# Query and key operands of two attention heads made on 128 partitions and put together by transfers

## The chip, the cores and the metric

The kernel runs on one core of a Trainium2 chip. The metric is the device time of one execution in microseconds (us), as the median of several runs. Times inside an execution come from one profiled execution; its span is counted from the first to the last instruction. TensorE is called PE, VectorE DVE, ScalarE ACT, GpSimd POOL and SyncE SP.

## The reference

One layer of a decoder with two kinds of attention side by side, for a sequence of 512 rows of width 1024, in float32:

```
h   = RMSNorm_pre(x)
[q_a|k_a|v_a|q_b|k_b|v_b] = h @ W_in
y_a = sliding-window attention with sinks + ALiBi   (8 query heads, 2 key/value heads, window 128)
y_b = differential attention + ALiBi                (4 heads, two 64-wide q/k each, 128-wide v)
x   = x + RMSNorm_post(concat(y_a, y_b) @ W_out)
x   = x + RMSNorm_post(W_down(gelu(g) * v)),  [g|v] = causal_dwconv3(RMSNorm_pre(x) @ W_up)
```

Scores are `q . k / 8 - slope * distance`, masked, then a softmax. All heads are 64 wide for queries and keys, so one projection of 128 columns holds two query heads, or the two keys of a differential head, or the two key heads of the window attention.

## The kernel before, in words

**Precision.** Every float32 matrix product is made from halves: an operand is rounded to a high part (`hi`, type float32r) and what is left is kept as a low part (`lo`). A general product takes three matmuls (hi·hi, lo·hi, hi·lo). In `split` and its like ACT makes the high part with a copy and DVE the low part with a subtraction.

**Scores.** `scores` (L387 to 390) makes a product of 64 channels with two matmuls instead of three, since PE has 128 rows: the query operand `q` holds in its 64 upper partitions the high part and in the 64 lower ones the low part of one head; the key operands `kh` and `kl` hold the high part, or the low part, of one head twice, in both halves. For the second head of a projection the high part lies in the lower partitions.

**How the operands are made.** A projection ends in `evac` (L340 to 346): DVE multiplies the sums by the reciprocal norms (L343), into a tile `pr` of 128 partitions (two heads of 64) and 512 columns, and hands it to one of two makers, each called once per head:

- `q_stack` (L369 to 375): ACT writes the scaled high part of 64 partitions (L373); DVE writes the scaled low part into the other 64 partitions (L374).
- `k_dup` (L377 to 385): ACT writes the high part of 64 partitions (L381), DVE the low part (L382); two transfers from SBUF to SBUF, issued by POOL (L383, L384, 64x512, 128 KB each), put the copies in the other 64 partitions.

`queries_a` and `keys_a` make the operands of the window attention (four query projections and one of keys), `queries_b` and `keys_b` those of the four differential heads (one of each per head). All operands come from a ring of 30 tiles of 128x512 (`a2`), taken and given back in order.

**What sets the order.** The attention is a list of steps: `swa_a` to `swa_c` for eight pairs of block and key head, then `diff_a` to `diff_e` for 16 pairs of head and block. Between steps `fill` takes pieces of work off a queue: the projections (`queue_projection`, L358 to 360, 24 matmuls each), the values (`queue_values`, L322 to 324) and later the output projection, so that PE has something to do while DVE and ACT work on the softmax. The framework then sorts the instructions of each engine by its own estimates, so that the order on an engine is not that of the text, and a small edit can move instructions in places that it does not touch. Each engine runs its list in order; an instruction that waits holds up all behind it on that engine.

**Other lines that are spoken of.** L389 and L390 are the two matmuls of `scores`. DVE reads the scores in L539 (window) and L417 (differential), and scales them in L428 and L554. L444 and L568 are transposes of the probabilities on PE. L195, L199 to L210 and L220 make and spread a row's norm (the power L201 on POOL, L210 on DVE, L220 on PE). L476 on DVE ends a differential head and frees its PSUM bank. L119 and L898 (ACT) with L120 and L899 (DVE) split weights. `post_a` takes the mean square of the new rows (L642, L649 on ACT, L629 to L631 on POOL) and scales them (L648, L656 on DVE); `post_b` transposes them (L664). From about 220 us on the feed-forward part runs, which the change's functions do not touch.

Of the kernel before, what the change touches and what calls it, by code (L numbers as in the profile page):

```python
# [10 lines left out]
F32 = mybir.dt.float32  # L11
F32R = mybir.dt.float32r
AF = mybir.ActivationFunctionType
ALU = mybir.AluOpType
PSUM = bass.MemoryType.PSUM

P = 128
# [4 lines left out]
DH = 64  # L22
# [10 lines left out]
T2, T4, T8, F2 = 30, 5, 3, 9  # L33


PAD = 72

WARM = 8

# [19 lines left out]
def fl(t):  # L59
    return t.bitcast(F32)  # L60
# [16 lines left out]
def hymba_layer(ctx, tc, x, st, wv, wqk, w_out, w_up, w_down, conv, cols, lam_in, sinks, gpost, gffn, gfin, out):  # L77
    nc = tc.nc
    TT = nc.vector.tensor_tensor
    STT = nc.vector.scalar_tensor_tensor  # L80
    ACT = nc.scalar.activation

    def pool(name, bufs=1, side="left", **kw):
        return tc.tile_pool(name=name, bufs=bufs, side=side, **kw)

    const = ctx.enter_context(pool("const"))
# [13 lines left out]
    a2 = Arena(wk, T2, [P, S], F32R, "a2")  # L100
# [3 lines left out]
    t2 = a2.get  # L104
# [34 lines left out]

    const.tile([P, PAD], F32, name="pad")  # L140
    cols_sb = const.tile([P, 16], F32, name="cols_sb")
# [31 lines left out]
    q = [(wqk[i], {}) for i in range(10)]  # L173
# [2 lines left out]
    nv = 2 + 2 * V_AFTER  # L176
    jobs += v[0:3] + q[0:nv] + v[3:6] + q[nv:10] + o + [(w, dict(big=True)) for w, kw in o[4::-1]]
    W = Stream(jobs, 2)

    ones_r = const.tile([P, P], F32R, name="ones_r")  # L180
    nc.vector.tensor_copy(ones_r, ones)
# [54 lines left out]
    for k in range(NK):  # L236
# [4 lines left out]
        else:  # L241
            t = f2.get(), f2.get()
# [8 lines left out]
    for k, (xr, wr, held) in enumerate(sts):  # L251
        ACT(hTh[k], xr, AF.Copy, scale=g_in(k))
        STT(hTl[k], xr, g_in(k), fl(hTh[k]), ALU.mult, ALU.subtract)
        h, l = t2(), t2()
        ACT(h[:, 0:384], wr, AF.Copy)
        TT(l[:, 0:384], wr, fl(h[:, 0:384]), op=ALU.subtract)
        for j in range(3):
            c = slice(j * P, (j + 1) * P)
# [12 lines left out]
    nc.sync.dma_start(lam_sb, lam_in)  # L271
    W.prepare(2)
    for t in range(NT):
# [35 lines left out]
    def queue_values(batch):  # L309
        st = {}  # L310

        def job(t, part):
            if t == 0 and part == 0:
                st["w"] = [W.next() for _ in range(3)]
            if part == 0:
# [32 lines left out]
    def queue_projection(done):  # L348
        st = {}

        def job(u):
            if u == 0:
                st["w"], st["o"] = W.next(), banks.get()
            h, l = st["w"]
# [11 lines left out]

    halves = [(slice(0, DH), slice(DH, P)), (slice(DH, P), slice(0, DH))]

    def q_stack(pr, half, scale):  # L369

        q = t2()
        a, b = halves[half]
        ACT(q[a], pr[a], AF.Copy, scale=scale)  # L373
        STT(q[b], pr[a], scale, fl(q[a]), ALU.mult, ALU.subtract)  # L374
        return q

    def k_dup(pr, half):  # L377

        kh, kl = t2(), t2()
        a, b = halves[half]  # L380
        ACT(kh[a], pr[a], AF.Copy)  # L381
        TT(kl[a], pr[a], fl(kh[a]), op=ALU.subtract)  # L382
        nc.gpsimd.dma_start(kh[b], kh[a])  # L383
        nc.gpsimd.dma_start(kl[b], kl[a])  # L384
        return kh, kl

    def scores(o, q, kd, qs, ks):  # L387
        kh, kl = kd
# [8 lines left out]
    kdb, qsb, pts, soft, ys, zq = {}, {}, {}, {}, {}, {}  # L397
    blocks = [[0, 1, 2, 3]] * 3 + [[2, 3, 0, 1]]

    def keys_b(h, pr):  # L400
        kdb[h] = [k_dup(pr, 0), k_dup(pr, 1)]

    def queries_b(h, pr):
        c = 0.125 * 2.0 ** (5 + h)
        qsb[h] = [q_stack(pr, 0, c), q_stack(pr, 1, c)]

    def diff_a(h, i):
        w = (i + 1) * P
# [78 lines left out]
    def mix(ts_, c, first, last, t):  # L487
        if t == ts_[0]:
            wmix[ts_, c] = kept.pop(c) if c in kept else W.next()
            if ts_ == (2, 3) and c > 4:  # L490
# [180 lines left out]
    kda, qa = [], []  # L671

    def keys_a(pr):
        kda.extend([k_dup(pr, 0), k_dup(pr, 1)])

    def queries_a(c, pr):
        qa.extend([q_stack(pr, 0, 0.125 * 2.0 ** c), q_stack(pr, 1, 0.125 * 2.0 ** (c + 1))])

    def queue_head(h):
        queue_projection(partial(keys_b, h))  # L680
        queue_projection(partial(queries_b, h))
# [27 lines left out]
    nc.gpsimd.tensor_scalar(g_sub, cols_sb[:, 12:13], DIFF_V ** 0.5 * (1.0 - LAMBDA_INIT), 0.0, op0=ALU.mult, op1=ALU.add)  # L709

    evac(st_ps[0], keys_a)
    for c in range(2):
        evac(st_ps[1 + c], partial(queries_a, c))
    queue_values(0)
    for c in range(2, 4):
        queue_projection(partial(queries_a, c))
# [9 lines left out]
    for m in range(2):  # L726
        nc.vector.tensor_tensor_reduce(out=lprod[:, m], in0=lam_sb[:, 2 * m], in1=lam_sb[:, 2 * m + 1],
                                       scale=1.0, scalar=0.0, op0=ALU.mult, op1=ALU.add,
# [33 lines left out]
    for n in range(2, len(steps) + DEP):  # L762
        if n < len(steps):
            h, i = steps[n]
# [79 lines left out]
    def sum_copy(q, n):  # L844
        name, b = (("U", B11), ("W", B12), ("V", B22), ("Z", B21))[n]
        sums[name, q] = dram.tile([P, D], F32, tag=f"{name}{q}", name=f"{name}{q}")
        tc.keep_in_program_order(nc.sync.dma_start(sums[name, q], w_down[q, b]))

    def sum_add(q, n):
        name, b = (("U", B12), ("W", B22), ("V", "U"), ("Z", "V"))[n]  # L850
        src = w_down[q, b] if isinstance(b, int) else sums[b, q]
        tc.keep_in_program_order(nc.gpsimd.dma_start(sums[name, q], src, accum_op=ALU.add, max_dma_last_dim=8192))
# [9 lines left out]
    for t, i, j in ((t11, 0, 0), (t21, 1, 0), (t22, 1, 1), (t12, 0, 1)):  # L862
        h, l = h_of(i, j)
# [224 lines left out]
    def get2():  # L1088
        return [banks.get(), banks.get()]
# [4 lines left out]
    a = get2()  # L1094
# [3 lines left out]
    c = get2()  # L1098
# [3 lines left out]
    b = get2()  # L1102
# [109 lines left out]
```

## Time and profile before

| | |
|---|---|
| median of 3 runs | 725.46 us (725.34 to 725.89) |
| the profiled execution | 724.03 us; its span 722.3 us |
| PE busy | 701.9 us (97%) |
| DVE busy | 625.1 us (87%) |
| ACT busy | 446.3 us (62%) |
| POOL busy | 70.0 us (10%) |
| transfers of L383 and L384 | 20, of 128.0 KB, 2.7 us from issue to landing in the median |

A busy engine was in an instruction; time spent on a semaphore or in handing a transfer to its queue is not counted. PE's matmuls overlap, so that in a timeline the distance between starts tells what one costs, and its own duration is longer. An idle time with an arrow names what ended it.

### The profile page before, as it was taken

To read this page: it belongs to the slowest core of one execution; us is meant where nothing else is said; L and a number is where in the kernel's file an instruction comes from. 1 tells how busy PE (TensorE), PEld (TensorE's weight loads), DVE (VectorE), ACT (ScalarE), POOL (GpSimd) and SP (SyncE) were. 2 spreads that over 40 slices of the span, in tenths; PEclk is the share of its full clock that TensorE was granted. 3 is DMA by queue.
4 is the path that set the end of the run, shared out by engine and by line. 5 is a ranking of instruction groups with operands and counts; after the bars stand their busy time and mean duration, and the time that the engine had idled before them with its cause. 6 is when DMAs were issued, how large, how long until landed. Compare 5 with 4: busy or idle time off the path is not lost.

```text
span 722.3 us, 11314 instructions
## 1 busy us (share of the span) xinstructions
PE 701.9 (97%) x4164; PEld 619.7 (86%) x4164; DVE 625.1 (87%) x1050; ACT 446.3 (62%) x790; POOL 70.0 (10%) x126
## 2 busy tenths in 40 slices
PE   8999999899998999999999999999999899999995
PEld 7888888688788889899999999999998788888884
DVE  6599979999785799999999899899987999988983
ACT  6698867677564455665575556557565666656661
POOL 2100102010322200000000000000000000000301
PEclk9999999999999999999999999999999999999998
DMA  8622223245667866887677686777864656677631
GB/s 305 228 87 59 85 87 95 73 117 166 194 231 269 206 154 190 249 212 214 182 193 212 181 245 179 213 185 190 229 164 145 237 184 203 191 249 255 210 117 58
DMA packets 33351, 130.83 MB, mean 181 GB/s; under 512 B 4752, under 2 KB 5776, under 8 KB 30736
## 3 DMA queue, kind: packets, MB, share of 16 engines
q1 hardware_dynamic: 28240, 107.57, 44.8%
q0 software_dynamic: 4480, 20.45, 15.3%
q10 hardware_dynamic: 576, 2.10, 0.7%
q8 instruction: 32, 0.52, 0.3%
q14 instruction: 23, 0.19, 0.1%
HBM read 123.29 MB, written 37.75 MB: 223 GB/s over the span
## 4 chain that ended last, share of the span: by engine, by line
PE 63%; DVE 5%; issue 1%; ACT 0%; POOL 0%; POOLq 0%; ACTq 0%; DVEq 0%
PE bank L940 10%; PE bank L942 10%; PE bank L941 9%; PE bank L1056 7%; PE bank L1057 7%; PE bank L1055 7%; PE bank L695 4%; PE bank L696 4%; PE bank L697 4%; DVE ct L832 1%; DVE ct L833 1%; DVE act L864 1%; DVE wlo L120 0%; DVE wlo L899 0%; PE bank L664 0%
## 5 line engine op out<-in xcount | busy, mean ns | idle before, releaser
L119 ACT ACTIVATE whi<-wr 128x1024 fp32r<-128x1024 f32 (+1 forms) x81 | 85.4, 1056 | 66.8 <-PE bank L1056 47.3
L120 DVE TENSOR_TENSOR wlo<-wr,whi 128x1024 fp32r<-128x1024 f32 (+1 forms) x81 | 98.5, 1217 | 19.9 <-ACT whi L119 19.3
L1056 PE MATMUL bank<-whi,al 128*128 128x512 f32 x224 | 87.3, 390 | 1.5 <-DVE al L394 1.5
L1055 PE MATMUL bank<-whi,ah 128*128 128x512 f32 x224 | 87.0, 390 | 0.4 <-ACT ah L393 0.4
L1057 PE MATMUL bank<-wlo,ah 128*128 128x512 f32 x224 | 87.2, 389 | 0.0
L898 ACT ACTIVATE whi<-wr 128x1024 fp32r<-128x1024 f32 x60 | 63.1, 1056 | 34.8 <-PE bank L696 15.5
L899 DVE TENSOR_TENSOR wlo<-wr,whi 128x1024 fp32r<-128x1024 f32 x60 | 73.1, 1219 | 0.6 <-ACT whi L898 0.6
L940 PE MATMUL bank<-hTh,whi 128*128 128x256 f32 x252 | 72.6, 289 | 0.7 <-ACT ub L959 0.5
L941 PE MATMUL bank<-hTl,whi 128*128 128x256 f32 x252 | 71.0, 282 | 0.0
L942 PE MATMUL bank<-hTh,wlo 128*128 128x256 f32 x252 | 70.4, 283 | 0.0
L695 PE MATMUL bank<-hTh,whi 128*128 128x512 f32 (+1 forms) x160 | 60.8, 380 | 0.0
L696 PE MATMUL bank<-hTl,whi 128*128 128x512 f32 (+1 forms) x160 | 60.7, 380 | 0.0
L697 PE MATMUL bank<-hTh,wlo 128*128 128x512 f32 (+1 forms) x160 | 60.7, 379 | 0.0
L898 ACT ACTIVATE whi<-sm 128x1024 fp32r<-128x1024 f32 (+1 forms) x42 | 34.7, 840 | 39.7 <-PE bank L941 19.0
L940 PEld LDWEIGHTS bank<-hTh,whi 128*128 128x128 f32 x252 | 48.1, 191 | 4.2 <-ACT ub L959 3.5
L1056 PEld LDWEIGHTS bank<-whi,al 128*128 128x128 f32 x224 | 42.0, 188 | 10.7 <-DVE al L394 1.9
L1055 PEld LDWEIGHTS bank<-whi,ah 128*128 128x128 f32 x224 | 42.0, 188 | 9.8 <-ACT ah L393 0.8
L899 DVE TENSOR_TENSOR wlo<-sm,whi 128x512 fp32r<-128x512 f32 (+1 forms) x42 | 39.9, 955 | 11.5 <-ACT whi L898 11.3
L1057 PEld LDWEIGHTS bank<-wlo,ah 128*128 128x128 f32 x224 | 42.1, 188 | 8.5
L941 PEld LDWEIGHTS bank<-hTl,whi 128*128 128x128 f32 x252 | 48.2, 191 | 0.5
L942 PEld LDWEIGHTS bank<-hTh,wlo 128*128 128x128 f32 x252 | 47.8, 191 | 0.0
L697 PEld LDWEIGHTS bank<-hTh,wlo 128*128 128x128 f32 x160 | 30.1, 188 | 5.9 <-DVE wlo L899 0.2
(266 smaller groups left out, 2017.7 us busy)
## 6 DMA issues: line engine op xcount, KB each, us to landing
wr<-in_w_up SPq DMA_DIRECT2D x64, 512.0 KB, 3.9
wr<-in_w_down SPq DMA_DIRECT2D x24, 512.0 KB, 4.3
wr<-in_w_out SPq DMA_DIRECT2D x13, 512.0 KB, 3.8
wr<-in_wqk SPq DMA_DIRECT2D x10, 512.0 KB, 3.7
Z<-in_w_down SPq DMA_DIRECT2D x8, 512.0 KB, 5.1
U<-in_w_down SPq DMA_DIRECT2D x8, 512.0 KB, 5.3
W<-in_w_down SPq DMA_DIRECT2D x8, 512.0 KB, 6.5
V<-in_w_down SPq DMA_DIRECT2D x8, 512.0 KB, 4.8
```

Source lines behind the costliest of these rows:

```text
L120: TT(l, r, fl(h), op=ALU.subtract)
L695: nc.tensor.matmul(u[:, c0:c1], lhsT=h[:, c], rhs=hTh[k][:, c0:c1], start=(k == 0), stop=False)
L696: nc.tensor.matmul(u[:, c0:c1], lhsT=h[:, c], rhs=hTl[k][:, c0:c1], start=False, stop=False)
L697: nc.tensor.matmul(u[:, c0:c1], lhsT=l[:, c], rhs=hTh[k][:, c0:c1], start=False, stop=(k == NK - 1))
L898: ACT(h[:, 0:n], src, AF.Copy)
L899: TT(l[:, 0:n], src, fl(h[:, 0:n]), op=ALU.subtract)
L940: nc.tensor.matmul(o[:, 0:H], lhsT=wh[:, c], rhs=rh[:, k], start=first and k == 0, stop=False, skip_group_check=True)
L941: nc.tensor.matmul(o[:, 0:H], lhsT=wh[:, c], rhs=rl[:, k], start=False, stop=False, skip_group_check=True)
L942: nc.tensor.matmul(o[:, 0:H], lhsT=wl[:, c], rhs=rh[:, k], start=False, stop=k == 3, skip_group_check=True)
L1055: nc.tensor.matmul(o, lhsT=ah[:, j, rs], rhs=wh[:, cs], start=first and j == 0, stop=False, skip_group_check=True)
L1056: nc.tensor.matmul(o, lhsT=al[:, j, rs], rhs=wh[:, cs], start=False, stop=False, skip_group_check=True)
L1057: nc.tensor.matmul(o, lhsT=ah[:, j, rs], rhs=wl[:, cs], start=False, stop=last and j == 1, skip_group_check=True)
```

## The change

For two heads at once: ACT writes the high part of all 128 partitions, once into each of the two operand tiles. DVE makes the low part of all 128 partitions in one subtraction. What has to lie in the other half is moved by transfers of 64 partitions that POOL issues: for queries two transfers of low parts out of a tile that is then given back, for keys four (high and low part of both heads), with one more ACT copy of the low part for the second operand. The scale of the window attention's queries now differs between the halves of an instruction, so it comes from a small constant tile, `qscale`, which eight memsets on POOL fill. A padding tile is made smaller by as much.

```diff
-PAD = 72
+PAD = 64
...
+    qscale = const.tile([P, 4], F32, name="qscale")
+    for c in range(4):
+        for m in range(2):
+            nc.gpsimd.memset(qscale[m * DH:(m + 1) * DH, c:c + 1], 0.125 * 2.0 ** (c + m))
...
-    def q_stack(pr, half, scale):
-
-        q = t2()
-        a, b = halves[half]
-        ACT(q[a], pr[a], AF.Copy, scale=scale)
-        STT(q[b], pr[a], scale, fl(q[a]), ALU.mult, ALU.subtract)
+    def q_stack(pr, scale):
+
+        (a, b), q, l = halves[0], (t2(), t2()), t2()
+        for t in q:
+            ACT(t, pr, AF.Copy, scale=scale)
+        STT(l, pr, scale, fl(q[0]), ALU.mult, ALU.subtract)
+        nc.gpsimd.dma_start(q[0][b], l[a])
+        nc.gpsimd.dma_start(q[1][a], l[b])
+        a2.free(l)
         return q
 
-    def k_dup(pr, half):
-
-        kh, kl = t2(), t2()
-        a, b = halves[half]
-        ACT(kh[a], pr[a], AF.Copy)
-        TT(kl[a], pr[a], fl(kh[a]), op=ALU.subtract)
-        nc.gpsimd.dma_start(kh[b], kh[a])
-        nc.gpsimd.dma_start(kl[b], kl[a])
-        return kh, kl
+    def k_dup(pr):
+
+        (a, b), kh, kl = halves[0], (t2(), t2()), (t2(), t2())
+        for t in kh:
+            ACT(t, pr, AF.Copy)
+        TT(kl[0], pr, fl(kh[0]), op=ALU.subtract)
+        ACT(kl[1], fl(kl[0]), AF.Copy)
+        for t in kh, kl:
+            nc.gpsimd.dma_start(t[0][b], t[0][a])
+            nc.gpsimd.dma_start(t[1][a], t[1][b])
+        return list(zip(kh, kl))
...
     def keys_b(h, pr):
-        kdb[h] = [k_dup(pr, 0), k_dup(pr, 1)]
+        kdb[h] = k_dup(pr)
...
-        qsb[h] = [q_stack(pr, 0, c), q_stack(pr, 1, c)]
+        qsb[h] = q_stack(pr, c)
...
-        kda.extend([k_dup(pr, 0), k_dup(pr, 1)])
+        kda.extend(k_dup(pr))
 
     def queries_a(c, pr):
-        qa.extend([q_stack(pr, 0, 0.125 * 2.0 ** c), q_stack(pr, 1, 0.125 * 2.0 ** (c + 1))])
+        qa.extend(q_stack(pr, qscale[:, c:c + 1]))
```

The lines behind the change have other numbers: in the listings L322 to L324 become L328 to L330, L358 to L360 become L364 to L366, L389 and L390 become L400 and L401, L444 becomes L455, and L649, L653 and L898 become L660, L664 and L909.

**First listing: PE at the start of the attention.** The matmuls with `hTh` and `hTl` make values; those of tiles `a2...` are the first scores: `a226_118` is the first key's high part, `a20_92` the first query operand. Before:

```order
L322 MATMUL bank2_86<-whi_401,hTh_177 128x320
L389 MATMUL bank5_89<-a226_118,a20_92 128x256
L389 MATMUL bank4_88<-a226_118,a20_92 128x256
L323 MATMUL bank2_86<-whi_401,hTl_178 128x320
L324 MATMUL bank2_86<-wlo_402,hTh_177 128x320
L322 MATMUL bank2_86<-whi_401,hTh_177 128x320
L323 MATMUL bank2_86<-whi_401,hTl_178 128x320
L324 MATMUL bank2_86<-wlo_402,hTh_177 128x320
L389 MATMUL bank6_90<-a226_118,a22_94 128x256
```
With the change:

```order
L328 MATMUL bank2_86<-whi_412,hTh_186 128x320
L329 MATMUL bank2_86<-whi_412,hTl_187 128x320
L330 MATMUL bank2_86<-wlo_413,hTh_186 128x320
L400 MATMUL bank5_89<-a226_118,a20_92 128x256
L400 MATMUL bank4_88<-a226_118,a20_92 128x256
L328 MATMUL bank7_91<-whi_318,hTh_186 128x320
L329 MATMUL bank7_91<-whi_318,hTl_187 128x320
L330 MATMUL bank7_91<-wlo_319,hTh_186 128x320
L401 MATMUL bank5_89<-a228_120,a20_92 128x256
```
The five matmuls on `bank2_86` that stood behind the first two scores stand ahead of them now. Behind these two come matmuls for other values, on `bank7_91`, and then the product with the key's low part (`a228_120`); the scores of the third query operand (`a22_94`) are later.

**Second listing: PE in differential head 2.** The matmuls with `hTh` and `whi` are those of the next projection; into `bank1_85` the first of them can only start when L476 has given that bank back. Before:

```order
L444 MATMUL bank3_87<-ident_149,a42_124 128x128 x4
L389 MATMUL bank2_86<-a226_118,a22_94 128x256
L390 MATMUL bank2_86<-a227_119,a22_94 128x256
L389 MATMUL bank4_88<-a226_118,a22_94 128x256
L390 MATMUL bank4_88<-a227_119,a22_94 128x256
L389 MATMUL bank5_89<-a24_96,a23_95 128x256
L390 MATMUL bank5_89<-a25_97,a23_95 128x256
L389 MATMUL bank6_90<-a24_96,a23_95 128x256
L390 MATMUL bank6_90<-a25_97,a23_95 128x256
L358 MATMUL bank1_85<-hTh_177,whi_1390 128x512
L359 MATMUL bank1_85<-hTl_178,whi_1390 128x512
```
With the change:

```order
L455 MATMUL bank3_87<-ident_149,a42_124 128x128 x4
L364 MATMUL bank1_85<-hTh_186,whi_1405 128x512
L365 MATMUL bank1_85<-hTl_187,whi_1405 128x512
L366 MATMUL bank1_85<-hTh_186,wlo_1406 128x512
L364 MATMUL bank1_85<-hTh_186,whi_1405 128x512
L400 MATMUL bank2_86<-a22_94,a28_100 128x256
L401 MATMUL bank2_86<-a27_99,a28_100 128x256
L400 MATMUL bank4_88<-a22_94,a28_100 128x256
L401 MATMUL bank4_88<-a27_99,a28_100 128x256
L365 MATMUL bank1_85<-hTl_187,whi_1405 128x512
L366 MATMUL bank1_85<-hTh_186,wlo_1406 128x512
```
Four of the projection's matmuls, which stood behind the first scores, stand ahead of them now, and two more between the first and the second query operand's.

**Third listing: ACT behind the attention.** L649 (L660) takes the squares of the new rows for `post_a`; L898 (L909) is a weight's split. Before:

```order
L898 ACTIVATE whi<-wr 128x1024
L649 ACTIVATE f_131,r_2151<-a_123 128x512
L649 ACTIVATE f_129,r_2151<-a_123 128x512
L653 DMA x_2156<-a_123 128x1024
L642 ACTIVATE f_128,r<-bank_85 128x512
```
With the change:

```order
L660 ACTIVATE f_131,r_2168<-a_123 128x512
L909 ACTIVATE whi<-wr 128x1024
L660 ACTIVATE f_129,r_2168<-a_123 128x512
L664 DMA x_2173<-a_123 128x1024
L653 ACTIVATE f_128,r<-bank_85 128x512
```
One of the two squares has moved ahead of the weight's split.

## Rows read from the trace of the kernel before

**Rows 1.** Busy time and share of each engine, from the page

```profile
PE 701.9 (97%) x4164; PEld 619.7 (86%) x4164; DVE 625.1 (87%) x1050; ACT 446.3 (62%) x790; POOL 70.0 (10%) x126
```

**Rows 2.** Stretch, its length, busy PE, PEld, DVE, ACT, POOL, clock, DMA share, GB/s

```profile
40.00:165.00 125.00, 122.00 (x658) 103.14 (x657) 114.77 (x307) 96.05 (x236) 13.10 (x28) 1.00 0.32 89
40.00:60.00 20.00, 20.00 (x115) 17.34 (x114) 19.27 (x56) 19.55 (x51) 0.00 (x0) 1.00 0.33 100
125.00:145.00 20.00, 18.09 (x91) 14.27 (x90) 18.86 (x49) 13.33 (x32) 3.08 (x7) 1.00 0.30 80
```

**Rows 3.** Groups by line and form: busy us, mean ns; idle before, releaser

```profile
L373 ACT ACTIVATE a<-f 64x512 fp32r<-64x512 f32 x16 | 10.0, 627 | 0.6 <-DVE f L343 0.4
L374 DVE SCALAR_TENSOR_TENSOR a<-f,a 64x512 fp32r<-64x512 f32 x16 | 11.0, 686 | 0.5
L394 DVE TENSOR_TENSOR al<-act,ah 128x512 fp32r<-128x512 f32 x48 | 32.8, 684 | 0.0
L252 ACT ACTIVATE hTh<-a,cols_sb 128x512 fp32r<-128x512 f32 x5 | 3.6, 723 | 4.2 <-DMA a<-in_st 4.2
L384 POOL DMA_DIRECT2D a<-a x10 | 5.1, 516 | 1.3 <-DVE a L382 0.6 <-issue 0.4 <-DVE a L554 0.2
```

**Rows 4.** Line L383, whole span: its transfers' time from issue to landing

```profile
DMA to landing us min/median/max: 2.2/2.7/4.0
```

**Rows 5.** Line L383, 71 to 76 us: the same

```profile
DMA to landing us min/median/max: 3.6/3.8/4.0
```

**Rows 6.** Timelines, 30 to 37 us: start, us, engine, line [idle before <-releaser]

```profile
31.93 1.39 DVE L382 TENSOR_TENSOR a<-f,a 64x512 fp32r<-64x512 f32 x2
31.79 1.32 POOL L383 DMA_DIRECT2D a<-a  x2 [6.78 <-ACT a L381]
34.37 0.48 PE L389 MATMUL bank<-a,a 128*128 128x256 f32 x2
36.90 0.38 PE L389 MATMUL bank<-a,a 128*128 128x256 f32 x1 [0.24 <-DVE m L539]
```

**Rows 7.** Timelines of DVE and PE, 57 to 59 us

```profile
57.27 0.69 DVE L374 SCALAR_TENSOR_TENSOR a<-f,a 64x512 fp32r<-64x512 f32 x1
58.19 0.28 PE L389 MATMUL bank<-a,a 128*128 128x256 f32 x1
```

**Rows 8.** Timelines of DVE and PE, 115 to 122 us

```profile
115.86 1.40 DVE L374 SCALAR_TENSOR_TENSOR a<-f,a 64x512 fp32r<-64x512 f32 x2
117.23 0.28 PE L389 MATMUL bank<-a,a 128*128 128x256 f32 x1
121.21 0.50 PE L220 MATMUL bank<-a,ones_r 128*128 128x512 f32 x1 [0.47 <-DVE a L210]
```

**Rows 9.** Timelines of DVE and PE, 139 to 144 us

```profile
139.24 1.40 DVE L374 SCALAR_TENSOR_TENSOR a<-f,a 64x512 fp32r<-64x512 f32 x2
141.82 0.74 DVE L476 SCALAR_TENSOR_TENSOR f<-bank,g_sub,f 128x512 f32<-128x512 f32 x1
139.31 0.63 PE L444 MATMUL bank<-ident,a 128*128 128x128 f32 x4 [0.37 <-ACT a L373]
142.62 0.50 PE L358 MATMUL bank<-hTh,whi 128*128 128x512 f32 x1 [1.18 <-DVE f L476]
142.95 0.39 PE L359 MATMUL bank<-hTl,whi 128*128 128x512 f32 x1
143.18 0.40 PE L360 MATMUL bank<-hTh,wlo 128*128 128x512 f32 x1
```

**Rows 10.** Timelines of DVE and PE, 158 to 160 us

```profile
158.10 1.41 DVE L374 SCALAR_TENSOR_TENSOR a<-f,a 64x512 fp32r<-64x512 f32 x2
159.81 0.34 PE L389 MATMUL bank<-a,a 128*128 128x384 f32 x1
```

**Rows 11.** Timelines of ACT and PE, 214 to 219 us

```profile
214.31 1.06 ACT L898 ACTIVATE whi<-wr 128x1024 fp32r<-128x1024 f32 x1 [1.42 <-DMA wr<-in_w_up]
218.67 1.32 PE L664 MATMUL bank<-ident,f 128*128 128x128 f32 x8 [2.77 <-DVE f L656]
```

## The prediction

> **What bounds the kernel now.** I began with the page: TensorE (PE) is busy 97% of the span [rows 1], so time is gained only where it stands still, and lost wherever it is made to stand. Then the busy time by stretch, for the stretch in which queries and keys are made: from 40 to 165 us PE is busy 122.0 of 125 us, so only 3.0 us of idle PE can be given back there, whatever VectorE (DVE) saves. In 40 to 60 us PE never idles, with ScalarE (ACT) busy 19.55 and DVE 19.27 of 20. In 125 to 145 us PE idles 1.91 us and DVE is the busiest engine [rows 2]. The groups by line and form give prices [rows 3]; the landing times of the transfers [rows 4, 5] and the timelines around each first use of a new operand [rows 6 to 11] give the places. The profiled execution took 724.03 us, 1.43 below the median of the runs shown (725.46). I work out a difference against it and add that to the median; about 0.2% (1.45 us) can be told from no change.
>
> **What goes and what comes.** There are eight query and five key projections. On DVE a pair of 64-partition subtractions becomes one on 128 partitions. The 64x512 form of the query costs 0.686 us [rows 3], that of the key 0.69 (two in 1.39, [rows 6]), and a subtraction on 128 partitions 0.684 (L394, [rows 3]): twice the partitions cost no more. So DVE loses 8 x 0.69 + 5 x 0.69 = 9.0 us. ACT gets one more copy per key projection (5 x 0.63 = 3.2) and, for the four query projections whose scale now comes from a tile, 8 x (0.723 - 0.627) = 0.8 us: L252 is such an instruction [rows 3]. Of these 4.0 us only the 0.4 of the second group's queries lie in or near 40 to 60 us, where ACT is full; PE waits for nothing there [rows 2], so I cost them at nothing, and at 0.4 if that cover is gone. GpSimd (POOL) gets 16 transfers of 128 KB at 0.52 us to issue [rows 3], which are 8.3 us on an engine that is idle nine tenths of the time; the eight small memsets lie at the start, before anything waits on POOL. PE's instructions are the same.
>
> What matters is the path of a query. Before, its operand was ready when DVE finished. Now it is ready after DVE, an issue on POOL and a landing: by the median of the ten landings of L383, 2.7 us [rows 4], that is 2.7 us later for the first half-head and 3.2 for the second. The ends are 2.2 and 4.0 us [rows 4]. I take the median; only beside DVE's scaling of the window attention (L554) did landings reach 3.6 to 4.0 [rows 5]. The Trainium skill, page "DMA: Bandwidth & Descriptors", section "Anatomy of one DMA — SWDGE (gpsimd) path", puts a fixed 2.0 us and the bytes over 436 GB/s on such a transfer; for 131,072 bytes that makes an estimate of 2.3 us, and the sum below would then end 1.6 us lower, for 0.4 less at four places. The trace does not agree: the median there is 2.7.
>
> **Place by place.**
> - Start of attention. DVE begins the key subtraction at 31.93 [rows 6]; now one of 0.69, so it ends at 32.6, and the query's one ends at 33.4. POOL, which begins at 31.79 and takes 0.66 a transfer there [rows 6], has the other key half and this key half ahead, so the query's goes at 33.45 and lands at 36.15. PE reached the first scores at 34.37 [rows 6] and now first runs five matmuls more (320 columns, 0.14 each by the 0.23 of 512 columns, [rows 9]): 35.1. It stands 1.1 us; the wait of 0.24 on DVE at 36.90 falls away [rows 6], as DVE is relieved. **+0.8**, ends 0 and +2.2 (a landing of 4.0).
> - Second group of heads. The query's subtraction at 57.27 was used by PE at 58.19 [rows 7]. Now eight transposes (0.16 each, four in 0.63 at 139.31, [rows 9]) and a matmul come first, to about 59.7; the operand lands at 57.27 + 0.7 + 2.7 = 60.7 (3.5: 61.5), or earlier by as much as the subtraction moves up: in its new order DVE has it ahead of the scaling that stood beside it. **+0.5**, ends 0 and +1.8.
> - Differential head 0: its query is made more than 5 us before its use by the order; 0.
> - Head 1. DVE's query pair at 115.86 becomes one, ending at 116.6; landing 119.3 and 119.8. PE, which took the first scores at 117.23 [rows 8], now has four transposes (0.16 each) and seven 512-column matmuls (0.23) first: 117.23 + 2.25 = 119.5. So it fits. The two reductions' spread (L210), which PE awaited 0.47 us at 121.21 [rows 8], come earlier on DVE, as the scores do later; but the later scores then queue behind it, and L201 on POOL stands behind two transfers. **-0.2**, ends -0.6 and +1.
> - Head 2, where the second listing shows the order. Before, PE ran four transposes at 139.31, then the scores, and then waited 1.18 us for L476, until 142.62 [rows 9]. Now four projection matmuls come ahead of the scores and wait for L476 first. DVE's pair at 139.24 is one, so L476, which began at 141.82 [rows 9], ends 0.69 earlier at the most; I take 142.0. The four matmuls run to 143.1, with the landings (139.95 + 2.7 = 142.65) under them; six matmuls and eight scores end at about 144.6. Before, six matmuls and eight scores ended at 142.62 + 0.33 + 5 x 0.23 = 144.1 [rows 9]. The work that hid the wait is now behind it: **+0.5**, ends -1.2 and +1.8.
> - Head 3. The pair at 158.10 was used at 159.81 [rows 10]. PE has four more matmuls first: 160.7. One subtraction that moves ahead of another of 0.67 ends at about 158.15, lands at 160.85 and 161.4. **+0.3**, ends 0 and +1.6.
> - The rest of DVE's relief. In 125 to 145 us 1.91 - 1.18 = 0.7 us of idle PE remains [rows 2, 9], and DVE has a key's and a query's subtraction less in front of it: **-0.5**. In the rest of 40 to 165 us the idle is 3.0 - 1.91 - 0.47 = 0.6; half of it: **-0.3**.
> - Behind attention. ACT idled 1.42 us for a weight and then ran L898 at 214.31, 1.06 us, ahead of both squares of L649; PE waited 2.77 us, until 218.67, for what comes of them [rows 11]. Now one of the squares (third listing) goes into that idle time, so the second ends earlier by up to a square: **-0.4**, ends -0.75 and 0. What follows to the end is PE-bound, with the same instructions in the same order but for a few neighbours: 0.
>
> Sum: 0.8 + 0.5 - 0.2 + 0.5 + 0.3 - 0.5 - 0.3 - 0.4 = +0.7. **Forecast: 726.2 us**, inside what can't be told from no change.
>
> **The rivals.**
> - *Transfers land late (slower).* Four transfers of a key and two of a query stand in one POOL queue, and DVE's work goes on beside them. For it: at 71 to 76 us the landings took 3.6 to 4.0 [rows 5], and POOL's issue of one waited for L554 on DVE [rows 3]. At 3.5 us in the start, head 2 and head 3, each stands 0.8 longer: 0.7 + 2.4 = +3.1, **728.6**; at 4.0 in all four places 0.7 + 5.2 = +5.9. It leaves the band from a landing of 2.95 us on (three times 0.25). Against it: the shortest landing was 2.2 and half of the ten took 2.7 or less [rows 4]. The Trainium skill speaks for this rival (page "SBUF — State Buffer", section "SBUF: two separate sides", the box on DVE blocking a DMA): while VectorE runs certain fast copies, GpSimd can't write the descriptors of its transfers. The one wait on L554 agrees with it; no run so far shows how long a transfer is held.
> - *DVE's relief comes back whole (faster).* DVE's 9.0 us are three times PE's idle time from 40 to 165 us. If each wait was DVE's queue, and the landings stay under other matmuls, all 3.0 go, with 0.4 behind attention, and only the start costs 0.8: -2.6, **722.9**. For it: DVE is as busy as PE in 40 to 60 and busier in 125 to 145 [rows 2]. Against: head 2's order puts the covering work behind the wait.
> - *The change moves no load that counts (no change).* DVE's freed time turns into idle, the landings hide, and the time is that of before, **725.5**. For it: PE waits so little now that neither has much to act on [rows 2].
>
> **How the numbers follow.** The forecast has a chance of 0.30 and the rival without effect 0.11: together 0.41 for within 0.2%, as both lie in 724.0 to 726.9. Late landings 0.29, and 0.04 for slower by another wait: 0.33 for slower. The whole relief: 0.26 for faster. The likeliest case alone has 724.6 to 727.6, by the ends of its two dearest places. The range goes to the faster case at 722.9 and on the other side past 728.6 to 729.4, between landings of 3.5 and 4.0.
>
> **What would show it.** Right: PE waits about 1 us for a transfer near 35 us, where DVE had let it go; DVE is busy some 9 us less, ACT about 4 more; the queries' transfers land in 2.5 to 3 us; near 142 us PE waits for L476 ahead of the scores; and the wait at 218.67 is shorter. Wrong: waits of PE on transfers over 1 us at three or four places (late landings), or none at all with the idle of 40 to 165 us under 1 us (whole relief); or a difference that arises after 220 us, where I expect none.

## The result, and the profile after

The changed kernel takes 731.12 us (median of five runs, 729.90 to 733.41) against 725.46 before: 1.0083 times as long, with a 95% interval of 1.0064 to 1.0102. That is 5.7 us, where +0.7 was forecast. The profiled execution took 731.08 us with a span of 729.3, so the two profiles that are compared below lie 7.05 us apart, 1.4 more than the medians.

The page's busy time, which answers to [rows 1], and the busy time by stretch, with the columns of [rows 2]:

```profile
PE 703.2 (96%) x4164; PEld 621.0 (85%) x4164; DVE 617.2 (85%) x1037; ACT 446.2 (61%) x795; POOL 81.2 (11%) x150
```

```profile
40.00:165.00 125.00, 118.62 (x640) 100.84 (x640) 105.86 (x295) 94.03 (x241) 19.33 (x40) 0.99 0.38 100
40.00:60.00 20.00, 20.00 (x117) 17.47 (x117) 19.09 (x63) 19.16 (x57) 1.03 (x2) 1.00 0.29 87
125.00:145.00 20.00, 17.21 (x85) 13.69 (x83) 17.83 (x41) 13.58 (x31) 4.59 (x9) 0.96 0.36 90
```

DVE was relieved as planned, and PE stands still more, not less: 6.4 us in 40 to 165 us, where it was 3.0. Over the whole span DVE is busy 7.9 us less, of 9.0 forecast, and ACT as long as before, where 4 more were forecast. The clock of 0.96 in the last row, where 1.00 stood before, will be of use below. What a subtraction costs was foreseen. The rows of DVE's subtraction (L380 in the changed kernel), with the duration's minimum, median and maximum in ns and the times of the first and last:

```profile
L380 DVE SCALAR_TENSOR_TENSOR a<-f,qscale,a x4: 723/750/751, 32.5 to 61.0; 128x512 fp32r<-128x512 f32 x4
L380 DVE SCALAR_TENSOR_TENSOR a<-f,a x4: 669/684/692, 81.6 to 159.7; 128x512 fp32r<-128x512 f32 x4
```

Eight instructions do what sixteen of L374 did [rows 3], at 0.68 to 0.75 us each.

**Where the time comes from** is read off the starts of the same matmul in the two timelines (us, lines of the kernel before):

| matmul | before | after | later by |
|---|---|---|---|
| last of the values (L322) | 97.78 | 98.14 | 0.36 |
| first L461 in differential head 0's product | 123.98 | 124.56 | 0.58 |
| first L461 in head 1's | 147.48 | 149.29 | 1.81 |
| first L461 in head 2's | 169.01 | 173.41 | 4.40 |
| last of the output projection (L500) in the attention's steps | 212.19 | 217.07 | 4.88 |
| first of the product L940 | 259.13 | 263.23 | 4.10 |
| last of the product L940 | 553.86 | 557.98 | 4.12 |
| seventeenth of the product L1055 | 573.04 | 578.77 | 5.73 |
| last matmul | 714.35 | 720.09 | 5.74 |
| end of the span | 722.3 | 729.3 | 7.0 |

Four places make it: the scores of differential head 2 (1.2, ahead of head 1's product), those of head 3 (2.6, ahead of head 2's), a step between 558 and 579 us (1.6), and the very end (1.3), behind the last matmul. At head 3 the page's view of the timeline shows one stop; the rows are PE's, POOL's and SP's (SP issues the loads from HBM):

```profile
162.42 0.39 PE L512 MATMUL bank<-whi,a 128*128 128x512 f32 x1
165.16 0.41 PE L400 MATMUL bank<-a,a 128*128 128x384 f32 x1 [2.35 <-issue]
```

```profile
160.92 0.56 POOL L381 DMA_DIRECT2D a<-a  x1 [6.39 <-issue]
161.50 0.51 POOL L382 DMA_DIRECT2D a<-a  x1
```

```profile
159.76 0.33 SPq L118 DMA_DIRECT2D wr<-in_w_out  x1
160.48 2.11 SPq L650 DMA_DIRECT2D f<-in_x  x2
163.39 0.33 SPq L118 DMA_DIRECT2D wr<-in_w_out  x1
```

The scores, which answer to [rows 10], wait 2.35 us for the query's transfer, though the profile calls that wait "issue". It was issued at 160.92 and landed 4.1 us later, the second 4.5 us later (line L381 at 160 to 162 us, then L382):

```profile
DMA to landing us min/median/max: 4.1/4.1/4.1
```

```profile
DMA to landing us min/median/max: 4.5/4.5/4.5
```

Beside it four loads were in flight: two of 512 KB and two of 256 KB. DVE's rows there are the product of the sums with the norms (L349, the L343 of before), a weight's split and the query's subtraction; the last row is L343 in the kernel before:

```profile
157.91 0.68 DVE L349 TENSOR_TENSOR f<-bank,f 128x512 f32<-128x512 f32 x1
158.52 1.21 DVE L120 TENSOR_TENSOR wlo<-wr,whi 128x1024 fp32r<-128x1024 f32 x1
159.72 0.67 DVE L380 SCALAR_TENSOR_TENSOR a<-f,a 128x512 fp32r<-128x512 f32 x1
```

```profile
155.43 0.67 DVE L343 TENSOR_TENSOR f<-bank,f 128x512 f32<-128x512 f32 x1
```

At the head before, PE waited for L487 (L476 before) ahead of the scores, as was foreseen, and then went on at a lower clock; the last row is the stretch of 143 to 147 us with the columns of [rows 2]:

```profile
140.08 0.63 PE L455 MATMUL bank<-ident,a 128*128 128x128 f32 x4 [0.60 <-ACT a L379]
142.53 0.50 PE L364 MATMUL bank<-hTh,whi 128*128 128x512 f32 x1 [1.82 <-DVE f L487]
```

```profile
143.00:147.00 4.00, 3.94 (x16) 3.09 (x15) 2.38 (x9) 2.58 (x8) 0.51 (x1) 0.57 0.70 193
```

A granted clock of 0.57 as a mean over these 4 us says that PE ran most of them at 1.2 and not at 2.4 GHz: by an estimate 4 x 0.43 = 1.7 us lost.

### The profile page after: what moved, and what is told of

Read it like the earlier page. It is cut to its first block, busy times and chain, and to the rows that moved or that the text cites. A ratio compares the mean times of both kernels' runs of the same rounds, so it can differ in the third digit from the quotient of the medians.

```text
span 729.3 us, 11365 instructions
## 1 busy us (share of the span) xinstructions
PE 703.2 (96%) x4164; PEld 621.0 (85%) x4164; DVE 617.2 (85%) x1037; ACT 446.2 (61%) x795; POOL 81.2 (11%) x150
## 4 chain that ended last, share of the span: by engine, by line
PE 64%; DVE 2%; ACT 2%; issue 1%; POOL 0%; POOLq 0%; DVEq 0%; ACTq 0%
PE bank L951 10%; PE bank L953 9%; PE bank L952 9%; PE bank L1067 7%; PE bank L1068 7%; PE bank L1066 7%; PE bank L706 5%; PE bank L707 5%; PE bank L708 5%; ACT whi L909 1%; DVE wlo L120 0%; DVE ct L843 0%; ACT ub L970 0%; DVE ct L844 0%; PE bank L675 0%
## 5 line engine op out<-in xcount | busy, mean ns | idle before, releaser
L909 ACT ACTIVATE whi<-wr 128x1024 fp32r<-128x1024 f32 x60 | 63.1, 1056 | 36.3 <-PE bank L707 15.5
L909 ACT ACTIVATE whi<-sm 128x1024 fp32r<-128x1024 f32 (+1 forms) x42 | 34.7, 840 | 39.7 <-PE bank L952 19.0
```

Of the source, the lines that this page charges most:

```text
L909: ACT(h[:, 0:n], src, AF.Copy)
```

## The experiments

The theory after the result: the time is lost because the queries' operands now hang on transfers, and these land late because the DMA engines are busy with weight loads. Rivals: the keys' transfers; the order that the framework made of the changed kernel; DVE's work that holds POOL's transfers back; a loss at the start that is only handed on.

**Which part of the change.** Three kernels take the parts of the change apart, with the makers as in the diff above and the old `q_stack` beside them as `q_half`. The first is the kernel before with the new keys alone (keys_only):

```diff
-        kdb[h] = [k_dup(pr, 0), k_dup(pr, 1)]
+        kdb[h] = k_dup(pr)
```

The second is the changed kernel with the window attention's queries as before (swa_old):

```diff
-        qa.extend(q_stack(pr, qscale[:, c:c + 1]))
+        qa.extend([q_half(pr, 0, 0.125 * 2.0 ** c), q_half(pr, 1, 0.125 * 2.0 ** (c + 1))])
```

The third is the changed kernel with the differential heads' queries as before (diff_old):

```diff
-        qsb[h] = q_stack(pr, c)
+        qsb[h] = [q_half(pr, 0, c), q_half(pr, 1, c)]
```

> The new keys with the old queries: no transfer stands between a query and its first scores, five DVE subtractions fewer, ten key transfers more. Theory (the queries' landings are the loss): 724 to 726 us, a ratio of 0.998 to 1.001; PE waits on no transfer, and the clock stays at 1.00 from 28 to 205 us. Rival (the keys' transfers or the order that comes with them): 727.5 us or more.

> The change with the window attention's queries made as before; the differential heads' queries and all keys as in the change. Theory: the stops at the heads stay (about 0.9 us near 120, 2 near 142 with matmuls at the half clock behind it, 2.5 near 165), the one near 36 us goes: 728 to 731 us. Rival (the loss begins at the start of the attention and is only handed on): 725 to 727.

> The change with the differential heads' queries made as before; the window attention's queries and all keys as in the change. Theory: PE stops about 1.6 us near 36 us for a transfer and 0.8 near 67, gets part of it back by 110 us as in the changed kernel, and no stop of over 1 us for a transfer comes later: 725 to 727 us. Rival (the start is what costs): 728 or more.

Measured, as a ratio to the kernel before with its 95% interval: the keys alone 0.9979 (0.9963 to 0.9995), 723.93 us; without the new window queries 1.0068 (1.0048 to 1.0088), 730.58; without the new differential queries 1.0000 (0.9986 to 1.0014), 725.56. The times came out as the theories said, the keys' at the fast end. Not every stop did: with the keys alone PE stood 0.46 us at 36.30 for a key's transfer, where no such wait was expected, and in the third kernel the stop near 67 us was 0.36 us and not 0.8. (The first expectation counts ten key transfers more; there are none: a key projection had four before and has four now.) The order of PE fits this comparison well: up to the first differential head that of "swa_old" is the keys' alone, behind it that of the changed kernel, and with "diff_old" the other way round. So the keys are worth 0.2%, the window queries give 0.2% back (their two intervals overlap), and the differential heads' queries cost 0.8%, some 6 us. In the second kernel the stop at head 3 is longer still. Its row, and the landing that it waited for:

```profile
164.54 0.55 PE L408 MATMUL bank<-a,a 128*128 128x384 f32 x1 [3.31 <-issue]
```

```profile
DMA to landing us min/median/max: 5.1/5.1/5.1
```

**What a transfer costs by itself.** A kernel of its own issues 64x512 transfers from one half of the partitions to the other, each after the one before has landed: from POOL, from ACT's queue, two at once, with one or two 512 KB loads (issued just before, or just after, called "late"), and while DVE runs eight copies or subtractions of 128x512 in SBUF:

```diff
+            for i in range(loads):
+                nc.sync.dma_start(ws[i], w_out[(2 * rep + i) % NK])
+            for t in dst:
+                engine.dma_start(t[DH:P], src[0:DH])
+            if dve:
+                nc.vector.tensor_scalar(work[0], src.bitcast(F32), 1.0, None, op0=ALU.mult)
...
```

> Leaves the whole layer out: transfers of 64x512 between partitions alone, one kind after another, four times each. Theory (a transfer shares the DMA engines with a 512 KB load that is in flight, and lands about when that load does): alone 2.2 to 2.8 us from POOL; beside one load 3.4 to 4.8, also when the load is issued a little later; beside two loads about 2 us more; from ACT's queue beside a load as late as from POOL's; beside DVE copies no later than alone. Rival (DVE's fast copies hold POOL back): beside copies at least 1 us later than beside subtractions, and beside a load as fast as alone.

The view of DMA issues, with count, size and the median time in us from issue to landing:

```profile
two<-src_two POOLq DMA_DIRECT2D x8, 128.0 KB, 2.3
lone<-src_lone POOLq DMA_DIRECT2D x4, 128.0 KB, 2.2
act<-src_act ACTq DMA_DIRECT2D x4, 128.0 KB, 2.2
load<-src_load POOLq DMA_DIRECT2D x4, 128.0 KB, 3.6
late<-src_late POOLq DMA_DIRECT2D x4, 128.0 KB, 4.2
loads<-src_loads POOLq DMA_DIRECT2D x4, 128.0 KB, 5.0
actload<-src_actload ACTq DMA_DIRECT2D x4, 128.0 KB, 4.1
actloads<-src_actloads ACTq DMA_DIRECT2D x4, 128.0 KB, 5.2
copies<-src_copies POOLq DMA_DIRECT2D x4, 128.0 KB, 2.4
subs<-src_subs POOLq DMA_DIRECT2D x4, 128.0 KB, 2.2
```

A load in flight adds 1.4 to 2.0 us, from either queue, a second one 1.4 more from POOL's and 1.1 from ACT's, where about 2 were expected. DVE's copies add 0.2, and POOL's issue of the transfer takes 0.73 us beside them instead of 0.51. The formula of the Trainium skill (page "DMA: Bandwidth & Descriptors", section "Anatomy of one DMA — SWDGE (gpsimd) path"), by which 2.3 us is the estimate for this size, agrees with a transfer alone, 2.2 here. The Trainium skill (page "SBUF — State Buffer", section "SBUF: two separate sides") says in its box on DVE that fp32 copies from SBUF to SBUF keep GpSimd from writing descriptors; the rows agree, but the effect is small here, 2.4 against 2.2. ACT's queue beside such copies was not run; beside a load it gains nothing, 4.1 against 3.6.

**The loads taken away in the kernel itself.** Two pairs of kernels leave loads out, in the kernel before and in the changed one: first the thirteen of the output projection's weight, then also those of the first up-projection weights and of x. In the first pair the order on PE through head 3 is that of the kernels with the loads.

```diff
+        if fake:
+            view = lambda u: u.rearrange("p (c k) -> p c k", c=8)
+            same = ones.unsqueeze(1).to_broadcast([P, 8, P])
+            ACT(view(h), same, AF.Copy)
+            TT(view(l), same, view(fl(h)), op=ALU.subtract)
+            return (h, l, t) if big else (h, l)
...
-    o = [(w_out[k], {}) for k in range(NK)]
+    o = [(w_out[k], dict(fake=True)) for k in range(NK)]
...
```

> The kernel before, without the thirteen loads of the output projection's weight (512 KB each): its parts are split from a constant in SBUF instead, so the output projection's numbers are others. It is the measure for the next run. Theory: within 2 us of 725, as PE did not wait for these loads; the loads of x and of the next weights may start earlier.

> The changed kernel, likewise without the thirteen loads of the output projection's weight; PE's order is that of the changed kernel through head 3. Theory (the queries' transfers of heads 1 to 3 are late because these loads are in flight beside them): landings of 2.2 to 3 us at heads 1 and 2, so PE's stop near 120 us goes, and that near 165 us is under 1.5; 1 to 3.5 us above the run without the loads of the kernel before, against 5.7 with them. Rival (the order that puts work ahead of the scores, whatever the landing): still 5 us or more above.

> The kernel before, without the loads of the output projection's weight, of the first up-projection weights and of x behind the attention; constants in SBUF stand for them, so the numbers are others. It is the measure for the next run. Theory: a little under 722, the time without the output projection's loads alone.

> The changed kernel with the same loads left out; two loads of later weights move up, and one of them falls beside the query's transfers of head 1, none beside those of heads 2 and 3. Theory: landings of about 4 us at head 1 and of 2.2 to 2.8 at heads 2 and 3; the stop near 165 us is 0.3 to 1 us; 1 to 2.5 us above the run without these loads of the kernel before. Rival (the order alone): 3.5 us or more above, as with the output projection's loads left out, and a stop of over 1.3 us at head 3.

Measured: 722.02 and 725.61 us in the first pair, 721.57 and 725.68 in the second; 3.6 and 4.1 us apart, where 1 to 3.5 and 1 to 2.5 were expected and it is 5.7 with all loads. Each median has an interval of about 1 us to either side, so the step from 5.7 to 3.6 or 4.1 is not clear of noise; what the loads do is read from the traces. (The kernel before is itself 2.7 us faster without the thirteen loads, a ratio of 0.9957, where at most 2 were expected.) At head 2 of both pairs and at head 3 of the second the landings went as the theory said. In the second pair's changed kernel the first query transfer of head 1 (at 116 to 118 us, with a load of a later weight beside it), of head 2 (141 to 142.5) and of head 3 (160 to 162) landed after:

```profile
DMA to landing us min/median/max: 4.1/4.1/4.1
```

```profile
DMA to landing us min/median/max: 2.4/2.4/2.4
```

```profile
DMA to landing us min/median/max: 2.3/2.3/2.3
```

And the stop at head 3 follows the landing: 2.35 us with all loads (4.1 to landing), 1.45 with those of x alone (3.3), 0.47 with none (2.3), and 3.31 without the new window queries (5.1). PE's rows at that place, in the kernel without the output projection's loads and then in the one without any of them:

```profile
163.51 0.41 PE L406 MATMUL bank<-a,a 128*128 128x384 f32 x1 [1.45 <-DVE a L411]
```

```profile
163.39 0.41 PE L406 MATMUL bank<-a,a 128*128 128x384 f32 x1 [0.47 <-issue]
```

At head 1 a load stood beside the transfers in both changed kernels (4.1 us), so that the first pair's forecast for that head missed: a later load had moved into the place. The 4.1 us of the second pair are the time that the rival named, the order alone, though without the stop that was to go with it. The order can be told from the landing by the distance between the products of two heads (from the first L461, or its like, to the next head's). At head 2 all the changed kernels here run the same matmuls in the same order. Times in us; the landings are that of the second query transfer at head 2 and of the first at head 3:

| kernel | landing, head 2 | clock, 143 to 147 us | product of head 0 to head 1 | landing, head 3 | head 1 to head 2 |
|---|---|---|---|---|---|
| before | none | 1.00 | 23.50 | none | 21.53 |
| changed | 3.9 | 0.57 | 24.73 | 4.1 | 24.12 |
| changed, old window queries | 3.7 | 1.00 | 23.97 | 5.1 | 26.52 |
| changed, old query at head 3 | 4.3 | 1.00 | 24.53 | none | 22.36 |
| changed, first pair | 2.6 | 1.00 | 22.99 | 3.3 | 23.50 |
| changed, second pair | 2.6 | 0.57 | 24.51 | 2.3 | 22.15 |

With the clock at 1.00 the order gains 0.5 us at head 2 when the transfer lands early, and loses 0.5 and 1.0 when it lands late: PE then stands 0.74 and 1.20 us for it. Where the clock fell, the place loses 1.0 to 1.2 us with either landing. At head 3 an early landing leaves 0.6 us, and later ones more. (The 26.52 hold a stretch at a clock of 0.58 besides, from 164 to 168 us.) So the order by itself costs next to nothing at these two heads. What parts the second pair in its profiles is 0.8 us up to head 0's product, 1.0 to head 1's with the lower clock in it, 0.6 to head 2's, 0.4 from there to the last matmul, and the end of the program (below): 1.3 us.

**Head 3's query alone made as before:**

```diff
-        qsb[h] = q_stack(pr, c)
+        qsb[h] = [q_half(pr, 0, c), q_half(pr, 1, c)] if h == 3 else q_stack(pr, c)
```

> The changed kernel with the queries of the last differential head alone made as before. Theory: the stop near 165 us goes and nothing takes its place: 2 to 3 us under the changed kernel, 728 to 729.2. Rival (the time lost in heads 1 and 2 already sets the end): 730.5 or more.

Measured 728.80 us, 1.0059 (1.0033 to 1.0085): 2.3 us under the changed kernel, as the theory said, though the two intervals overlap. The trace shows the gain in its place: head 2's product starts at 170.55, where it is 173.41 in the changed kernel, and PE has no stop of over 0.6 us at head 3. At head 2 PE waits for the second transfer of the query:

```profile
145.08 0.36 PE L408 MATMUL bank<-a,a 128*128 128x256 f32 x1 [1.20 <-DMA a<-a]
```

**The transfers in another queue:**

```diff
-        nc.gpsimd.dma_start(q[0][b], l[a])
-        nc.gpsimd.dma_start(q[1][a], l[b])
+        nc.sync.dma_start(fl(q[0][b]), fl(l[a]))
+        nc.sync.dma_start(fl(q[1][a]), fl(l[b]))
```

> The changed kernel with the queries' transfers issued by SP instead of POOL, in the queue that issues the weight loads; at heads 2 and 3 its order has them ahead of the next load. Theory: where no load is in flight when they are issued they land in 2.2 to 2.8 us, and the loads behind them come later instead, so the stop near 165 us is under 1 us: 726 to 729. Rival (POOL's making of the transfers is what takes long): the stops go everywhere, 725 or less. Other rival (the loads that now wait for the queries are missed later): 731 or more, with PE, ACT or DVE waiting for weights.

Measured 724.65 us, 1.0008 (0.9994 to 1.0023): as fast as before, and faster than expected. But not by faster landings: head 3's took 4.6 us (issued at 158.59), and PE still waited 1.25 us for it. The framework put the transfers earlier and the scores later, and POOL's end is shorter by the 1.3 us. At head 2 the landings took 4.0 and 3.8 us, and PE stood only 0.29 us for them, since ten projection matmuls now stand ahead of the scores; from head 0's product to head 1's it takes 21.52 us, 3.2 less than in the changed kernel, where the lower clock is in it. So a late landing costs what the order does not cover. How the 6.5 us that it gains on the changed kernel divide between order and transfers stays open.

**The low parts moved by ACT instead of transfers**, for the differential heads alone (cross) and for all queries (cross_all), with the new keys in both:

```diff
-        nc.gpsimd.dma_start(q[0][b], l[a])
-        nc.gpsimd.dma_start(q[1][a], l[b])
+        ACT(q[0][b], fl(l[a]), AF.Copy)
+        ACT(q[1][a], fl(l[b]), AF.Copy)
```

> New keys; window queries as before; for the differential heads the one subtraction on 128 partitions, but the low parts are put into the other half by two ACT copies of 64x512 instead of two transfers. Theory: the operand is ready about 1.2 us later than before and not 2.2 to 4.8, with nothing of it hanging on the DMA engines: no stop of over 0.8 us for a query, 723 to 726. Rival (any delay of the query costs it): 728 or more.

> New keys; for all queries one subtraction on 128 partitions and two ACT copies of 64x512 in place of the transfers. Theory: the window part pays, since ACT has 0.45 us free of 20 between 40 and 60 us and gets 1.3 us more per projection: 0.5 to 2.5 us above the version that does this for the differential heads alone, 723.6 to 725.6. Rival (DVE's relief counts for more there): 722.5 or less.

Measured 723.09 us, 0.9982 (0.9969 to 0.9996), and 726.72, 1.0031 (1.0019 to 1.0043). The first beats both kernels, like the keys alone. It is also the measure for the transfers: beside the kernel with the old window queries (swa_old, 1.0068) it differs in the text only in how the low parts get into the other half, by copies or by transfers, and that is 0.9% or 7.5 us. The order on PE at the heads differs too. The second lost more than expected, at the place that was named: in 40 to 60 us ACT is busy 19.75 of 20, and PE, which never idled there [rows 2], stood 2.1 us for a split that ACT and DVE came to late:

```profile
40.00:60.00 20.00, 17.85 (x104) 15.67 (x104) 19.03 (x61) 19.75 (x57) 0.00 (x0) 1.00 0.29 80
```

```profile
47.22 0.50 PE L596 MATMUL bank<-a,Va 128*128 128x512 f32 x1 [2.15 <-DVE a L405]
```

**The end of the program.** The last matmul of the changed kernel is 5.74 us late, its end 7.0. Between them POOL's own last step, a drain, is longer. From the last line's instructions (minimum, median and maximum in ns, and when), before, after, and in the run without new differential queries:

```profile
L1208 POOLq DRAIN  x3: 46/93/5244, 716.2 to 722.0; - x3
```

```profile
L1219 POOLq DRAIN  x3: 46/102/6555, 722.0 to 729.0; - x3
```

```profile
L1227 POOLq DRAIN  x3: 46/93/5902, 714.7 to 721.1; - x3
```

With all that POOL issued counted, 36 transfers (the kernel of transfers alone) made it 3.73 us, 56 (before) 5.24, 64 5.90, 70 6.39, 72 (after) 6.56: 0.08 us for each. To tell the count from the lateness of the queries, sixteen transfers that nobody waits for were added to the kernel before:

```diff
-    const.tile([P, PAD], F32, name="pad")
+    pad = const.tile([P, PAD], F32, name="pad")
+    nc.vector.memset(pad, 0.0)
...
+    for i in range(16):
+        nc.gpsimd.dma_start(pad[DH:P, 4 * i:4 * i + 4], fl(hTh[NK - 1])[0:DH, P + 4 * i:P + 4 * i + 4])
```

> The kernel before with sixteen more transfers issued by POOL (64 partitions of 16 bytes, into a padding tile that nobody reads), where POOL is idle from about 224 to 239 us; the order on PE is unchanged. Theory (each transfer that POOL issues lengthens the last step of the program on POOL by 0.082 us, whatever its size, and nothing else comes after): the profile's POOL step at the end takes 6.55 us instead of 5.24, and the kernel is 1.0 to 1.6 us slower, a ratio of 1.0014 to 1.0022. Rival (the longer step belongs to the late queries or to the size of the transfers): 5.24 us at the end and no difference.

```profile
L1211 POOLq DRAIN  x3: 46/102/6555, 717.0 to 724.1; - x3
```

The same 6.555 us as in the changed kernel, and a ratio of 1.0020 (1.0008 to 1.0032), 726.04 us against 724.87 on the same chip. These transfers carry 1 KB each, so it is their number that counts, not their size.

## Why the prediction was wrong

The step that failed is the price of a query's way from DVE to PE: 2.7 us for the landing and nothing for the issue. Measured are 3.9 to 4.5 us for the transfers that PE had to wait for behind the start, each with a load beside it, and 0.3 to 0.5 us from the end of the subtraction to the issue. It weighs most in the term for head 3. Two more things were not in the sum, the clock and the end of the program. Term by term:

- **The start, forecast +0.8.** The landing at 36.15 was 36.60, the stop 1.63 us instead of 1.1. But at 97.8 us PE is only 0.36 late, the second group's stop included: what lies between gives most of both back.
- **Second group of heads, +0.5.** PE stood 0.62 us at 66.80, where a transfer landed at 66.7, 3.9 us after its issue. The profile names DVE's reading of the scores instead, which ended at the same time; in the runs without the new differential queries, of all heads or of head 3, it names the transfer at this place (0.36 and 0.52 us). Right in size.
- **Head 1, -0.2.** The wait for L210 went, as said. In its place PE stood 0.72 us at 120.73 for the query's transfer, 4.1 us to landing and not 2.7: the table's second and third row differ by 0.2, so +0.2.
- **Head 2, +0.5.** The order did what the second listing let expect: PE waits 1.82 us for L487 ahead of the scores. Measured are 1.2 us, with the lower clock behind that stop in it, which was no term of the sum. In the runs with an even clock the place loses 0.5 and 1.0 us for another reason (table above): the second transfer lands 3.7 and 4.3 us after its issue, and not under the matmuls as the forecast had it. With a landing of 2.6 us it gains 0.5.
- **Head 3, +0.3.** This is the step that failed most: 2.6 us. The operand was to land at 160.85 and landed at 165.02, 4.2 us later. 1.8 of these PE was late already at head 1's product. The subtraction came 0.4 late beside that: it ended at 160.4 and not at 158.15, as the product of sums and norms that it takes its input from ran at 157.91 and no longer at 155.43 (a weight's split stood between the two in both kernels). The issue followed 0.5 us later, which the sum had at nothing, and the landing took 4.1 us in place of 2.7.
- **DVE's relief, -0.8.** It exists: with the new keys alone PE is 1.51 us later than before at head 0's product and 0.30 at head 1's, so 1.2 us are gained between them. In the changed kernel the stops take its place.
- **Behind attention, -0.4.** PE waited 2.88 us at 223.66 for L667, against 2.77 [rows 11]: nothing gained there. The row of the table that seems to show a gain (4.88 to 4.10) goes with the clock: the kernel before ran at 0.57 in 219.5 to 223.5 us, the changed one at 1.00; the other step, at 558 to 579 us, is a like stretch of the changed kernel at 0.59 (566 to 570 us). Together they add 0.85 us; no instruction of the change stands at either place.
- **What was not in the sum:** 1.3 us at the end, 0.08 for each of the 16 transfers from POOL. The engine was costed as idle nine tenths of the time; its queue has a price at the end, where POOL is the last.

The mechanism that the forecast put second, transfers that land late, is what happened at head 3, and in part at head 2. That its price at a landing of 4.0 us (5.9 us) is near the 5.7 measured is luck: it has 1.3 us more at each of four places, while the start gave most of its wait back, and the end and the clock, which it does not have, make up for that. It was given too little because of one reading: the landings of 3.6 to 4.0 us at 71 to 76 us [rows 5] were laid to DVE's scaling L554, which stood beside one of the four issues. SP had issued a 512 KB load at 70.82. (One more of the ten took 3.7 us, at 108 us, beside the other transfers of its key and without L554.) The price that was taken for heads 1 to 3, the median of ten transfers, was for the most part that of transfers with no load beside them, while each of these heads takes a load of the output projection.

## What to carry to other kernels

A transfer that replaces an engine's write makes the operand wait for an issue and a landing, and the landing takes longer beside loads. Price it by the landing beside those loads (here 4 us, not 2.2), at each place where it will be used, set against the work that the order puts ahead of that use, and look what else is in flight there before another cause is named. Data that were already made by transfers, as the keys here, can have their arithmetic widened at no such price. Count the transfers of a queue whose engine ends last.

## What the runs showed of the hardware

- Each transfer that POOL issues lengthens POOL's drain at the end of the program by 0.08 us (3.73 us for 36, 5.24 for 56, 6.56 for 72, and as much for sixteen more of 1 KB as for sixteen more of 128 KB); in these kernels that is the last thing to end, so sixteen cost 1.3 us.
- A 128 KB transfer between partitions takes 2.2 us alone, 3.6 to 4.2 beside one load of 512 KB and 5.0 to 5.2 beside two, from POOL's queue and from ACT's.
- The profiles hold short stretches at the lower clock behind a stop of PE, 4 us at 0.57 to 0.59, which by an estimate (4 us times the missing share) cost 1.6 to 1.7 us each, but not behind the same stop: at 220 us before, at 143 and at 566 in the changed kernel, and none behind the 2.35 us at head 3. Behind the same stop of 1.8 us at head 2, in the same order, the clock fell in two of the five changed kernels of the table above and stayed at 1.00 in three. The changed kernel's profile has one such stretch more than that of before, and it is further from it than the medians are, by 1.4 us (7.05 against 5.7). What decides at which stop the clock falls was not settled; where two profiles differ by 1.5 us, these stretches are to be looked for first.
